# Head sums of k squared as four products of 128 tokens in place of one product of 512 tokens, in a two-layer RWKV-7 and neighbourhood-attention trunk

## Chip, cores and metric

The kernel runs on one core of one Trainium2 chip. The metric is device time in microseconds (us) of one execution; lower is better. The time before is a median of 1630.3 us of three runs (1628.93 to 1637.69).

## What is computed

Two sequences of 512 tokens with 1024 channels (16 heads of 64) go through two layers. Layer 0 is bidirectional RWKV-7 time mixing, layer 1 a gated 2-D neighbourhood attention. The change lies in the first lines of layer 0, where `k` is scaled and divided by its length, head by head:

```python
k = heads(lerp(1) @ w_k).astype(f32)
...
kk = k * k_k.astype(f32).reshape(N_HEADS, HEAD_DIM)
kk = kk / jnp.maximum(jnp.sqrt(jnp.sum(kk * kk, axis=-1, keepdims=True)), 1e-12)
```

So for each of the 16 heads and each of the 512 tokens one sum of 64 squares is needed. The scan that follows uses `-kk` and `kk * a`:

```python
def step(s, inp):
    r_t, w_t, k_t, v_t, a_t, b_t = inp
    sa = jnp.einsum('bhvk,bhk->bhv', s, a_t)
    s = s * w_t[:, :, None, :] + sa[..., None] * b_t[:, :, None, :] + v_t[..., None] * k_t[:, :, None, :]
    return s, jnp.einsum('bhvk,bhk->bhv', s, r_t)
```

## The kernel before, in words

Activations lie with channels on partitions: a tile is 128 channels (two heads) by 512 tokens. A float32 weight product is made of three products of float32r halves, so a *column* (128 output channels) is 8 triples of matmuls, one triple for each 128 input channels. Sequence 0 and 1 are called s = 0 and s = 1, and p = 0..7 counts the columns of a weight.

**The head sums.** `column(s, "k", p, ps)` takes the finished column of `k` from PSUM, copies it and stores it (L717, L718), squares it with the scale `k_k` on ACT (L726), and then lets TensorE (PE) sum the squares over the partitions of each head: one float32 matmul whose weights are the two columns of `ssel` (a one for each partition of head 0, and of head 1), and whose moving operand is the whole square, 128 x 512 (L730). A float32 matmul runs as two passes, so the trace has two records for each. The result, 2 rows by 512 tokens, lies in a PSUM bank of the tag `pm`; ACT copies it out (L733), and the SP queue stores it in the DRAM buffer `ss` of 16 rows (L736). After p = 7 the 16 x 512 sums are loaded as 128 x 64 (L742), ACT takes the root (L744), DVE bounds it and takes the reciprocal (L746, L747), and SP stores it as `rn` (L749). Every `prep` of that sequence then loads rows of `rn` (L955).

There are 8 such sums for s = 0 and 8 for s = 1, in two quite different places:

- **s = 0** lies before the scan. `run` (L1843, L1844) walks through the columns z and k of sequence 0 and lets the `prelude` of sequence 1 step along. There the Tile framework's scheduler sets the order on each engine. Then come the operands for the first columns of r (`shifted`, L1846).
- **s = 1** lies inside `scan_phase`, under a manual schedule for PE, DVE and ACT. There a program of the kernel's own, `weave` (L1703), sets the order at build time. It holds some 15 threads (generators): the recurrence (64 *steps*; each todo n, that is a sequence and four heads, has 8 of them), `preps`, `elimination` and `merges` (they make the inverse matrices of one todo), `finish`, and `flow`. `flow` feeds a long list of weight columns that the scan doesn't depend on at once, to fill PE: `products` (L887 to L889), with their loads, splits and operands, in the groups r, v of s = 0, k of s = 1 (here the head sums), low-rank and z of s = 1, r and v of s = 1, w_o of s = 0, the rest of z, and the first 24 columns of w_in. A triple of L887, L888, L889 is called a filler here; 672 of them are in the scan.

`weave` picks the next instruction by a planner, the class `Clock`: it holds a time for each engine and a cost for each instruction (`matmul` for PE, `scalar` for ACT), and takes the thread of best rank among those that could start now. Where none can start for over 300 ns (`WARM`) and PE was planned busy for under 70% of the last 3.4 us (`cool`), it puts in a *spare* matmul (L1729), whose result nobody reads and which keeps the TensorE clock up. So a change in the cost of one instruction can change the order of all that follows. The recurrence of todo n starts a step with L1277 and then waits, in its first step, until the inverse of todo n is there: that is in steps 9, 17, 25, 33, 41 and 49, and in these waits PE has nothing but fillers, preps and spares.

A group's operands are eight pairs of tiles (`act`, 18 buffers of half a pair each), so the pairs of the next group can only be made as the last column of a group gives its own back. The first column of a group therefore waits on ACT and DVE (L832, L834; in the last group L844 to L872).

Of the kernel before, what the change touches and what calls it, by code (L numbers as in the profile page):

```python
# [13 lines left out]
AF = mybir.ActivationFunctionType  # L14
# [5 lines left out]
P = 128  # L20
T = 512
# [21 lines left out]
CC = {}  # L43
# [7 lines left out]
class Clock:  # L51
# [41 lines left out]
    def room(self, key, bufs):  # L93
        s = self.slots.get(key, ())
        return 0.0 if len(s) < bufs else min(self.left(n) for n in s)
# [88 lines left out]
    def matmul(self, i, ins, n, t):  # L184
        f32, tr = ins[0].dtype == F32, bool(i.is_transpose)
        ts, tp = tuple(i.tile_size), tuple(i.tile_position)
        if not f32:
            c = 0.4375 * n + 3
        elif tr:
            c = 0.84 * n + 2  # L190
        elif ts == (128, 128):
            c = max(1.73 * n + 1, 100.0)
        else:
            c = max(53.0, 0.875 * n + 2)
        if self.mode != ts and self.tiles:
            t = max([t] + [x + 100.0 for x in self.tiles.values()])
            self.tiles = {}
        full = ts == (128, 128)
        if full and not tr and self.mode not in (None, ts):
            c += 104.0  # L200
        elif not full and self.mode == (128, 128):
            t += 48.0
        self.mode = ts
        for (r, q), x in self.tiles.items():
            if r == tp[0] or q != tp[1]:
                t = max(t, x)
        self.tiles[tp] = t + c
        self.t["P"] = t + (13.0 if f32 and not tr else 6.5)
        return t, t + c + self.LAT["P"]
# [44 lines left out]
class Trunk:  # L254
# [111 lines left out]
    def consts(self):  # L366
        nc, cp = self.nc, self.cp
        self.cc = cp.tile([P, NCC], F32, tag="cc", name="cc")
        nc.sync.dma_start(self.cc, self.a["const"])
        c = lambda n, w: self.cc[:, CC[n]:CC[n] + w]  # L370
        self.ident, self.bones, self.ssel = c("ident", 128), c("bones", 128), c("ssel", 2)
        if self.SUMS:
            self.bones = cp.tile([P, 128], F32R, tag="sel", name="sel")
            nc.scalar.copy(self.bones, c("bones", 128))
        self.mstrict, self.mr = c("mstrict", 64), (c("mr", 64), self.cc[:, CC["mr"] + 64:CC["mr"] + 128])
        self.scan = (c("scan", T), self.cc[:, CC["scan"] + 1:CC["scan"] + 1 + T])
        w = c("win", 64)
        self.lower = bass.AP(tensor=w.tensor, offset=w.offset + 31, ap=[list(w.ap[0]), [-1, 32], [1, 32]])
        self.ones = cp.tile([P, P], F32, tag="ones", name="ones")
        nc.vector.memset(self.ones, 1.0)  # L380
        self.one = self.ones[:, 0:1]
        self.dv = dv = cp.tile([P, 136], F32, tag="dv", name="dv")
        v = lambda n, w, o=0: self.cv[:, CV[n] + o:CV[n] + o + w]
        ts = nc.vector.tensor_scalar
        ts(dv[:, 0:16], v("w0", 16), 0.5, None, op0=ALU.mult)
        ts(dv[:, 16:32], v("a0", 16), -0.5, None, op0=ALU.mult)
        ts(dv[:, 32:40], v("ka", 8), -0.5, None, op0=ALU.mult)
        ts(dv[:, 40:48], v("ka", 8), -0.5, 1.0, op0=ALU.mult, op1=ALU.add)
        ts(dv[:, 48:56], v("bin", 8), 0.125, None, op0=ALU.mult)
        ts(dv[:, 56:64], v("bin", 8, 24), 0.5, None, op0=ALU.mult)  # L390
        ts(dv[:, 64:72], v("bin", 8, 16), 0.5, None, op0=ALU.mult)
        ts(dv[:, 72:80], v("lnw", 8), 0.5, None, op0=ALU.mult)
        ts(dv[:, 80:88], v("lnb", 8), 0.5, None, op0=ALU.mult)
        ts(dv[:, 88:112], v("mu", 24), 0.5, None, op0=ALU.mult)
        ts(dv[:, 112:136], v("mu", 24), -1.0, 1.0, op0=ALU.mult, op1=ALU.add)
# [296 lines left out]
    def column(self, s, kind, p, ps):  # L692

        nc, sp = self.nc, self.sp
        vt, act = nc.vector, nc.scalar
        first = lambda e: (e, None, lambda c, n=ps.tensor.name: c.at([n]))
        keep, whole = self.clock.keep, ps.tensor.name
        if kind == "z":

            o, th = self.tmp(), self.tmp()  # L700
            if s == 0:
                yield first("D")
                vt.tensor_tensor(o, ps, self.rstd0, op=ALU.mult)
                ps = o
            yield "A" if s == 0 else first("A")
            keep.add(whole)
            act.activation(th, ps, AF.Tanh, scale=0.5)
            yield "D"
            keep.discard(whole)
            vt.scalar_tensor_tensor(o, th, 1.0, ps, op0=ALU.add, op1=ALU.mult)  # L710
            self.save("z", s, p, o)
            return
        yield "A", None, lambda c: max(c.at([ps.tensor.name]), min(c.room(("tmp", id(self.main)), self.NTMP), 1e10))
        o = self.tmp()
        if kind == "k":
            keep.add(whole)
        act.copy(o, ps)  # L717
        self.save(kind, s, p, o)  # L718
        if kind == "r":
            self.made.add((kind, s, p))  # L720
            return
        if kind == "k":
            yield "A"
            keep.discard(whole)
            sq = self.tmp()
            act.activation(sq, ps, AF.Square, scale=self.vec("kk", p))  # L726
            free, room = self.bank()
            yield "P", free, lambda c: max(room(c), c.at([sq.tensor.name]))
            ss = self.p("pm", (2, T))
            nc.tensor.matmul(ss, self.ssel, sq, start=True, stop=True)  # L730
            yield "A"
            row = self.tmp((2, T))
            act.copy(row, ss)  # L733
            if p == 0:
                sp["ss", s] = self.dram(f"ss{s}", (16, T))
            self.load(sp["ss", s][2 * p:2 * p + 2], row)  # L736
            self.made.add((kind, s, p))
            if p == NP - 1:
                yield "S", None, lambda c: c.at([sp["ss", s].tensor.name])

                rn = self.tmp((P, 64))
                self.load(rn, sp["ss", s].rearrange("a (b c) -> (a b) c", b=8))  # L742
                yield "A"
                act.activation(rn, rn, AF.Sqrt)  # L744
                yield "D"
                vt.tensor_scalar(rn, rn, 1e-12, 2.0 ** 0.5, op0=ALU.max, op1=ALU.mult)  # L746
                vt.reciprocal(rn, rn)  # L747
                sp["rn", s, 0] = self.dram(f"rn{s}", (16, T))
                self.load(sp["rn", s, 0].rearrange("a (b c) -> (a b) c", b=8), rn)  # L749
                self.made.add(("rn", s))  # L750
            return

        if p == 0:

            sp["vt", s] = self.dram(f"vt{s}", (4, 2, NCH // 2, 2, L, 2, 2, HD))
        yield "A"
        back = self.tmp()
        act.copy(back, o[:, ::-1])
        for d in range(2):
            free, room = self.bank()  # L760
            yield "P", free, lambda c: max(room(c), c.at([back.tensor.name]))
            vp = self.p("pm")
            for m in range(4):
                nc.tensor.transpose(vp[:, m * P:(m + 1) * P], (back if d else o)[:, m * P:(m + 1) * P], self.ident)
            yield "A", None, lambda c: max(c.at([vp.tensor.name]), c.room(("vs", id(self.main)), self.NVS))
            vs = self.t("vs", (P, 4, P), self.NVS)
            act.copy(vs, vp.rearrange("p (m c) -> p m c", m=4))
            for j in range(2):
                self.store("vt").dma_start(
                    sp["vt", s][p // 2, j, :, :, :, d, p % 2].rearrange("m h t c -> t (m h) c"),  # L770
                    vs[64 * j:64 * j + 64].rearrange("t m (h c) -> t (m h) c", h=2))
        self.made.add((kind, s, p))
# [1249 lines left out]
```

## Time and profile before

| | |
|---|---|
| median of 3 runs | 1630.3 us |
| profiled execution, device time | 1627.3 us |
| its span, first to last instruction | 1625.5 us |
| granted TensorE clock, mean | 0.981 of full |
| PE busy, 18748 matmul records | 1533.3 us, 94% of the span |
| DVE busy | 1218.4 us, 75% |
| ACT busy | 983.7 us, 61% |
| data moved | 340.46 MB, mean 209 GB/s |
| L1729 spares | 124 records, 62 matmuls |

All times in the text on the profile are of this one execution. A row of a timeline reads: start in us, us from the first start to the last end, engine, line, operation, output <- inputs, tile size (rows*columns of the array), shape, count, and in brackets the idle time before it and who ended it. A row of a table by stretches gives for each engine the busy time and (x) the records, then the granted TensorE clock, the share of the DMA engines and GB/s.

### The profile page before, as it was taken

To read this page: it belongs to the slowest core of one execution; us is meant where nothing else is said; L and a number is where in the kernel's file an instruction comes from. 1 tells how busy PE (TensorE), PEld (TensorE's weight loads), DVE (VectorE), ACT (ScalarE), POOL (GpSimd) and SP (SyncE) were. 2 spreads that over 40 slices of the span, in tenths; PEclk is the share of its full clock that TensorE was granted. 3 is DMA by queue.
4 is the path that set the end of the run, shared out by engine and by line. 5 is a ranking of instruction groups with operands and counts; after the bars stand their busy time and mean duration, and the time that the engine had idled before them with its cause. 6 is when DMAs were issued, how large, how long until landed. Compare 5 with 4: busy or idle time off the path is not lost.

```text
span 1625.5 us, 46341 instructions
## 1 busy us (share of the span) xinstructions
PE 1533.3 (94%) x18748; PEld 1178.7 (73%) x18748; DVE 1218.4 (75%) x2714; ACT 983.7 (61%) x1949; POOL 179.2 (11%) x336
## 2 busy tenths in 40 slices
PE   7989999899989998988999999999999999999998
PEld 6866776666667676766677777777777788777776
DVE  8986587689778787876899998656676575754664
ACT  6567565757648456675666655544667665555562
POOL 0001124201011012231000011000000002100000
PEclk9989999999899999999999999999999999999999
DMA  6447687867576777677776775567664256645553
GB/s 242 158 169 260 212 279 237 270 195 245 167 251 227 239 248 218 224 242 242 247 262 212 233 262 180 160 191 245 196 226 155 93 162 223 224 165 185 163 162 104
DMA packets 182006, 340.46 MB, mean 209 GB/s; under 512 B 25344, under 2 KB 58240, under 8 KB 181792
## 3 DMA queue, kind: packets, MB, share of 16 engines
q1 hardware_dynamic: 158144, 256.75, 49.5%
q0 software_dynamic: 23648, 80.76, 13.9%
q8 instruction: 147, 2.41, 0.6%
q14 instruction: 67, 0.55, 0.1%
HBM read 230.33 MB, written 107.09 MB: 208 GB/s over the span
## 4 chain that ended last, share of the span: by engine, by line
PE 70%; DVE 11%; DMA 7%; issue 5%; ACT 5%; SPq 1%; DVEq 0%; POOL 0%; ACTq 0%; POOLq 0%
PE pm L887 8%; PE pg L454 7%; PE pg L455 6%; PE pg L456 6%; PE pm L888 6%; PE pm L889 6%; PE pf L1199 3%; DMA dab<-ab 2%; PE sc L1537 2%; PE po L1570 2%; PE us L1318 2%; PE pt L1555 2%; PE zy L1271 2%; PE us L1298 2%; DVE ab L1021 1%
## 5 line engine op out<-in xcount | busy, mean ns | idle before, releaser
L887 PE MATMUL pm<-act,whi 128*128 128x512 f32 x672 | 294.6, 438 | 2.7 <-ACT act L832 1.0
L888 PE MATMUL pm<-act,whi 128*128 128x512 f32 x672 | 268.0, 399 | 7.7 <-DVE act L834 6.8
L889 PE MATMUL pm<-act,wlo 128*128 128x512 f32 x672 | 267.3, 398 | 6.6 <-DVE wlo L808 6.6
L887 PEld LDWEIGHTS pm<-act,whi 128*128 128x128 f32 x672 | 127.7, 190 | 45.3 <-issue 12.2
L454 PE MATMUL pg<-act,whi 128*128 128x512 f32 x384 | 160.3, 418 | 0.0
L889 PEld LDWEIGHTS pm<-act,wlo 128*128 128x128 f32 x672 | 128.1, 191 | 37.2 <-DVE wlo L808 8.5
L888 PEld LDWEIGHTS pm<-act,whi 128*128 128x128 f32 x672 | 128.4, 191 | 33.9 <-DVE act L834 11.8
L455 PE MATMUL pg<-act,whi 128*128 128x512 f32 x384 | 152.8, 398 | 0.0
L456 PE MATMUL pg<-act,wlo 128*128 128x512 f32 x384 | 152.3, 397 | 0.0
L404 DVE TENSOR_TENSOR wlo<-raw,whi 128x512 fp32r<-128x512 f32 x148 | 101.6, 689 | 56.1 <-ACT whi L403 55.7
L403 ACT CAST whi<-raw 128x512 fp32r<-128x512 f32 x148 | 91.7, 619 | 83.0 <-PE pg L455 64.9
L808 DVE TENSOR_TENSOR wlo<-raw,whi 128x512 fp32r<-128x512 f32 x168 | 114.6, 684 | 29.1 <-ACT whi L806 29.1
L806 ACT CAST whi<-raw 128x512 fp32r<-128x512 f32 x168 | 103.8, 621 | 45.7 <-PE pm L888 39.5
L456 PEld LDWEIGHTS pg<-act,wlo 128*128 128x128 f32 x384 | 72.2, 188 | 14.9 <-issue 0.3
L454 PEld LDWEIGHTS pg<-act,whi 128*128 128x128 f32 x384 | 72.3, 188 | 14.4 <-issue 3.3
L1098 DVE TENSOR_TENSOR N<-etmp,N 128x30 f32<-128x30 f32 (+14 forms) x240 | 78.9, 329 | 4.6
L455 PEld LDWEIGHTS pg<-act,whi 128*128 128x128 f32 x384 | 72.5, 189 | 13.5 <-issue 2.8
L1096 DVE TENSOR_TENSOR etmp<-N 128x30 f32<-128x30 f32 (+14 forms) x240 | 78.8, 328 | 4.6
L1199 PE MATMUL pf<-cab 64*64 64x128 f32 (+1 forms) x2048 | 68.5, 268 | 6.3 <-issue 5.9
L1551 ACT ACTIVATE sb<-sb,mx 128x256 f32<-128x256 f32 x128 | 64.5, 506 | 11.4 <-DVE mx L1550 10.4
L1548 DVE CUSTOM_DVE_ANT_0 sb<-sc,bias 128x256 f32<-128x256 f32 x128 | 50.1, 420 | 24.3 <-PE pt L1555 13.3
L1310 ACT COPY X<-us 64x256 f32<-64x256 f32 x128 | 47.1, 368 | 33.5 <-PE zy L1177 31.7
(391 smaller groups left out, 3531.3 us busy)
## 6 DMA issues: line engine op xcount, KB each, us to landing
dab<-ab POOLq DMA_DIRECT2D x32, 1024.0 KB, 7.4
cab<-dab SPq DMA_DIRECT2D x64, 512.0 KB
raw<-in_w_in_dram SPq DMA_DIRECT2D x128, 256.0 KB
bias<-in_rpb_dram SPq DMA_DIRECT2D x32, 384.0 KB
raw<-in_w_z_dram SPq DMA_DIRECT2D x32, 256.0 KB
raw<-in_w_k_dram SPq DMA_DIRECT2D x32, 256.0 KB
raw<-in_w_r_dram SPq DMA_DIRECT2D x32, 256.0 KB
k<-dk SPq DMA_DIRECT2D x32, 256.0 KB
```

Of the source, the lines that this page charges most:

```text
L403: self.nc.scalar.copy(hi, src)
L404: (eng or self.nc.vector).tensor_tensor(lo, src, hi.bitcast(F32), op=ALU.subtract)
L454: nc.tensor.matmul(ps, hi, x[k][0], start=(k == 0), stop=False)
L455: nc.tensor.matmul(ps, hi, x[k][1], start=False, stop=False)
L456: self.mm = nc.tensor.matmul(ps, lo, x[k][0], start=False, stop=(k == KT - 1))
L806: nc.scalar.copy(hi, raw[h])
L808: nc.vector.tensor_tensor(lo, raw.pop(h), hi.bitcast(F32), op=ALU.subtract)
L887: nc.tensor.matmul(ps, hi[:, at], xh, start=(k == 0), stop=False)
L888: nc.tensor.matmul(ps, hi[:, at], xl, start=False, stop=False)
L889: nc.tensor.matmul(ps, lo[:, at], xh, start=False, stop=(k == KT - 1))
L1098: vt.tensor_tensor(N[:, q + 1:, :q], tv, N[:, q + 1:, :q], op=ALU.add)
L1199: end = nc.tensor.matmul(st.f[half(a), h, 0, d, g] if st.last else st.f[half(a), h, :, d, g], ab[half(h), d, g, 2 * e[d] + 1 - a], rt if s ...
```

## The change

The weights become 32 columns of the constant `bones` (0.5 where partition and column belong to the same head): columns 48 to 79, 16 of head 0 and 16 of head 1. The square is cut into four pieces of 128 tokens, and each piece gets its own matmul, whose 32 result rows go to PSUM partitions 32j to 32j+31; so four column groups of the array are used in place of one. The PSUM tile and the copy become 128 x 128, SP's store takes every 16th row (8 rows of 128 tokens) and puts them back in token order, and the missing factor 2 goes into the scale of the root. `Clock.matmul` gets a new case, too: a matmul in a 128 x 32 tile is costed like one in a full tile (1.73 ns per token of a row, at least 100), no longer by 0.875 ns per token. The constant `ssel` stays in the table, unused.

```diff
@@ Clock.matmul
-        elif ts == (128, 128):
+        elif ts in ((128, 128), (128, 32)):
             c = max(1.73 * n + 1, 100.0)
         else:
             c = max(53.0, 0.875 * n + 2)
@@ Trunk.consts
-        self.ident, self.bones, self.ssel = c("ident", 128), c("bones", 128), c("ssel", 2)
+        self.ident, self.bones, self.ssel = c("ident", 128), c("bones", 128), self.cc[:, CC["bones"] + 48:CC["bones"] + 80]
@@ Trunk.column
-            ss = self.p("pm", (2, T))
-            nc.tensor.matmul(ss, self.ssel, sq, start=True, stop=True)
+            ss = self.p("pm", (P, P))
+            for j in range(4):
+                nc.tensor.matmul(ss[32 * j:32 * j + 32], self.ssel, sq[:, j * P:(j + 1) * P], start=True, stop=True)
             yield "A"
-            row = self.tmp((2, T))
+            row = self.tmp((P, P))
             act.copy(row, ss)
             if p == 0:
                 sp["ss", s] = self.dram(f"ss{s}", (16, T))
-            self.load(sp["ss", s][2 * p:2 * p + 2], row)
+            self.load(sp["ss", s][2 * p:2 * p + 2].rearrange("a (j t) -> j a t", j=4), row[0:P:16])
@@ after the last p
-                act.activation(rn, rn, AF.Sqrt)
+                act.activation(rn, rn, AF.Sqrt, scale=2.0)
```

The order of instructions shows how the change moves the program. (Lines behind L730 have a number higher by one in the changed kernel: its L888 is L887 of before, its L1730 is L1729.) On PE in the k columns of sequence 0, before:

```order
L456 MATMUL zy_1041<-act_964,wlo_1038 128x512
L730 MATMUL pm_1021<-tmp_1019,cc 2x512
L454 MATMUL zy_1122<-act_915,whi_1114 128x512
L455 MATMUL zy_1122<-act_914,whi_1114 128x512
L456 MATMUL zy_1122<-act_915,wlo_1115 128x512
```

And now:

```order
L456 MATMUL zy_1044<-act_964,wlo_1041 128x512
L731 MATMUL pm_1021<-tmp_1019,cc 32x128 x4
L454 MATMUL zy_1128<-act_915,whi_1120 128x512
L455 MATMUL zy_1128<-act_914,whi_1120 128x512
L456 MATMUL zy_1128<-act_915,wlo_1121 128x512
```

Here nothing moved on PE: four matmuls stand where one stood. In the scan the order differs from the first head sum of s = 1 on. The largest difference stands at the first column of the last group, w_in, that is at the 481st to 488th filler. Before, PE reaches it in steps 44 to 46, with the recurrence between its triples (its last triple, and what follows):

```order
L1199 MATMUL pf_13030<-cab_418_1582 64x2x64 x16
L887 MATMUL pm_12817<-act_13003,whi_12634 128x512
L888 MATMUL pm_12817<-act_13002,whi_12634 128x512
L889 MATMUL pm_12817<-act_13003,wlo_12635 128x512
L1318 MATMUL us_13013<-X_12810,Tm_13008 64x64 x8
L1322 MATMUL zy_12966<-X_12810,R_13005 64x64 x8
```

Now PE reaches it in step 49, while the recurrence waits for the inverse of todo 6, and its last triples stand between spares (L1730) and the products of a prep (L978, L979):

```order
L1730 MATMUL zy_13348<-cc 128x256 x3
L978 MATMUL pm_13441<-h_1419_7116,w2h_13336 128x512
L979 MATMUL pm_13441<-h_1419_7116,w2l_13335 128x512
L1730 MATMUL zy_13348<-cc 128x256
L978 MATMUL pm_13450<-h_1443_7285,w2h_13336 128x512
L979 MATMUL pm_13450<-h_1443_7285,w2l_13335 128x512
L1730 MATMUL zy_13348<-cc 128x256 x9
L888 MATMUL pm_13382<-act_13494,whi_13082 128x512
L889 MATMUL pm_13382<-act_13493,whi_13082 128x512
L890 MATMUL pm_13382<-act_13494,wlo_13083 128x512
L1730 MATMUL zy_13348<-cc 128x256 x5
```

So the boundary between the last two groups moved out of the steps into a wait, and 19 spares were planned there (one more follows behind these rows). In the whole program the spares go from 62 to 87.

## The prediction, made before the changed kernel ran

> **What bounds the kernel now.** I read the page's busy times and its chain first, then the head sums by their lines, then the timeline around them, and last the long waits of the scan by stretches.
>
> ```profile
> PE 1533.3 (94%) x18748; PEld 1178.7 (73%) x18748; DVE 1218.4 (75%) x2714; ACT 983.7 (61%) x1949; POOL 179.2 (11%) x336
> PE 70%; DVE 11%; DMA 7%; issue 5%; ACT 5%; SPq 1%; DVEq 0%; POOL 0%; ACTq 0%; POOLq 0%
> ```
>
> PE is the bound over the whole: busy 94%, and 70% of the chain that ends last. So the time can be written as PE's useful work plus PE's lost time (idle, spares, half clock). The change must be judged by both. The head sums themselves:
>
> ```profile
> L730 PEld LDWEIGHTS pm<-tmp,cc x32: 80/82/84, 103.2 to 407.0; 128*2 128x2 f32 x32
> L730 PE MATMUL pm<-tmp,cc x32: 591/592/1061, 103.2 to 407.4; 128*2 128x512 f32 x32
> L733 ACT COPY tmp<-pm 2x512 f32<-2x512 f32 x16 | 9.2, 573 | 11.5 <-PE pm L730 11.5
> ```
>
> All 32 passes lie between 103 and 408 us. A pass is 592 ns long, but passes overlap, so what one sum takes from PE is read from the starts around it. Four rows of the timeline at the second sum of s = 0:
>
> ```profile
> 107.02 0.39 PE L454 MATMUL zy<-act,whi 128*128 128x512 f32 x1
> 107.25 0.39 PE L455 MATMUL zy<-act,whi 128*128 128x512 f32 x1
> 107.56 1.02 PE L730 MATMUL pm<-tmp,cc 128*2 128x512 f32 x2
> 108.51 0.50 PE L454 MATMUL zy<-act,whi 128*128 128x512 f32 x1
> 108.85 0.40 PE L455 MATMUL zy<-act,whi 128*128 128x512 f32 x1
> ```
>
> Neighbours start every 0.23 us (107.02 to 107.25). From 107.25 to 108.85 are 1.60 us where two such gaps would be 0.46: the sum costs PE 1.14 us. Its two passes start 1.02 - 0.59 = 0.43 apart, so 0.86 is streaming of 2 x 512 tokens, and 0.28 is the way into the small tile and out of it.
>
> **The four products.** Whether they run side by side can be read from other lines of this kernel:
>
> ```profile
> 301.01 1.06 PE L1199 MATMUL pf<-cab 64*64 64x128 f32 x32
> ...
> 1211.47 1.09 PE L1570 MATMUL po<-pts,vtok 128*64 128x128 f32 x16
> 1212.49 1.13 PE L1537 MATMUL sc<-k,q 64*128 64x256 f32 x8
> 1213.56 0.87 PE L1555 MATMUL pt<-cc,sb 128*128 128x128 f32 x6
> ```
>
> The length of one pass of each, from the rows by line:
>
> ```profile
> L1199 PE MATMUL pf<-cab x2048: 218/269/418, 250.5 to 1090.5; 64*64 64x128 f32 x163, 64*64 64x64 f32 x24
> ```
>
> ```profile
> L1570 PEld LDWEIGHTS po<-pts,vtok x512: 132/137/137, 1151.4 to 1585.1; 128*64 128x64 f32 x171
> L1570 PE MATMUL po<-pts,vtok x512: 272/273/324, 1151.4 to 1585.2; 128*64 128x128 f32 x171
> ```
>
> ```profile
> L1555 PE MATMUL pt<-cc,sb x256: 270/272/329, 1142.0 to 1579.1; 128*128 128x128 f32 x128
> ```
>
> L1555 fills the array: 6 passes of 128 tokens, each 0.27 long, start over 0.87 - 0.27 = 0.60, or 0.12 each. L1570 writes two column groups in turn: 16 passes start over 0.82. As 8 pairs that is 0.117 a pair; one after the other it would be 0.05 a pass, which no pass of 128 tokens has here. L1199 uses four tiles, and its 32 passes start over 0.79: eight fours, 0.113 each. So a slot of about 0.115 us takes one pass from each tile. Four column groups are not in the trace, but two and a two-by-two are, and I take two slots: 2 x 0.115 = 0.23, plus 0.28 for in and out, is 0.51 us in place of 1.14. Bounds: in pairs (four slots) 0.74, one after the other (eight) 1.2. So a sum gains 0.63 us, with ends 0.40 and -0.06.
>
> Each pass has a weight load of its own. Sixteen loads of L1570, of 137 ns, would be 2.2 us in a row, and the call took 1.02 (1211.47 to 1212.49); so loads hide behind passes. The Trainium skill, "TensorE: Matmul & The Clock Gate", Part 3, section "The mechanism", says otherwise: a load overlaps a running matmul only where its row group is another one, and four column tiles share their rows. By that rule eight loads of 82 ns would stand between the passes, a sum would cost 0.28 + 0.23 + 0.66 = 1.17, and nothing would be gained; the trace's call of L1570, also in one row group, speaks against it.
>
> **ACT.** The copy goes from 2 x 512 to 128 x 128. The nearest rows:
>
> ```profile
> L1283 ACT COPY Z<-zy 128x256 f32<-128x256 f32 x64 | 23.9, 373 | 38.2 <-PE zy L1277 37.8
> ...
> L1005 ACT COPY wc<-e 128x8 f32<-128x8 f32 x32 | 6.2, 193 | 0.0
> ```
>
> Between 193 ns at 8 elements and 373 at 256, 128 is about 280: 0.29 us less for each of 16. ACT is busy 61%; this counts only where ACT is the next in line (below). The root with a scale costs nothing: it is the same instruction. SP's store has 8 rows of 512 bytes where it had 2 of 2 KB, at most some tenths of a us, on a path only for the last p of each sequence. I put it at nothing.
>
> **s = 0, before the scan.**
>
> ```profile
> 100.00:140.00 40.00, 37.68 (x148) 25.36 (x148) 30.26 (x47) 27.69 (x49) 1.81 (x1) 1.00 0.80 275
> ...
> 147.65 1.87 PE L730 MATMUL pm<-tmp,cc 128*2 128x512 f32 x2 [3.73 <-ACT tmp L726]
> 149.45 4.61 PE L1729 MATMUL zy<-cc 128*128 128x256 f32 x12
> 149.56 0.58 ACT L733 COPY tmp<-pm 2x512 f32<-2x512 f32 x1 [0.32 <-PE pm L730]
> ```
>
> PE is busy 37.68 of 40 us, but the DMA engines are at 0.80, more than in any of the scan's waits below (0.66 to 0.74), so PE's 7 x 0.63 = 4.4 us may be eaten by weights that come late. The last sum ran at half clock after an idle PE: 1.87 us would become about half of that. But behind it PE runs spares until 153.7: it waits for the operands of the first r column, which ACT and DVE make one after the other, not for the sum. There ACT is next in line, and it gains 2 x 0.29. So s = 0 gains between 0.6 us (ACT alone) and 5 us; I take 2.5.
>
> **s = 1, in the scan.** Eight sums at 0.63 are 5.0 us less work for PE. That is all of it that the edit says itself. But the planner puts 87 spares in place of 62, 25 more, and none of these 25 lies ahead of the first sum of s = 1. What a spare stands for is read from the six long waits, from the L1277 of steps 9, 17, 25, 33, 41 and 49 to that of the next step (PE, PEld, DVE, ACT, POOL busy, clock, DMA):
>
> ```profile
> 356.20:433.30 77.10, 71.26 (x802) 49.31 (x806) 65.00 (x126) 48.27 (x86) 9.88 (x17) 0.91 0.67 215
> 487.90:528.10 40.20, 39.68 (x656) 31.59 (x660) 35.65 (x54) 32.68 (x60) 7.26 (x12) 1.00 0.69 226
> 578.50:645.80 67.30, 61.17 (x850) 46.52 (x853) 55.38 (x100) 41.51 (x78) 12.30 (x20) 0.95 0.73 239
> 696.20:741.90 45.70, 39.45 (x597) 30.04 (x599) 34.47 (x57) 32.82 (x59) 14.31 (x22) 0.96 0.66 210
> 799.80:874.70 74.90, 70.27 (x839) 53.78 (x842) 69.81 (x134) 50.48 (x84) 6.98 (x11) 0.98 0.74 247
> 925.80:999.00 73.20, 71.72 (x913) 56.97 (x916) 69.11 (x130) 45.00 (x79) 11.40 (x19) 1.00 0.70 227
> ```
>
> The same six stretches, L1729 alone:
>
> ```profile
> 356.20:433.30 77.10, 4.31 (x16) 2.86 (x16) 0.91 0.67 215
> 487.90:528.10 40.20, 0.00 (x0) 0.00 (x0) 1.00 0.69 226
> 578.50:645.80 67.30, 7.83 (x28) 6.16 (x28) 0.95 0.73 239
> 696.20:741.90 45.70, 2.49 (x10) 1.81 (x10) 0.96 0.66 210
> 799.80:874.70 74.90, 4.55 (x14) 3.13 (x14) 0.98 0.74 247
> 925.80:999.00 73.20, 0.00 (x0) 0.00 (x0) 1.00 0.70 227
> ```
>
> Four waits hold spares: 68 records, 34 spares, 19.2 us. In the same four PE is idle (the stretch less PE's busy time) for 5.8, 6.1, 6.3 and 4.6 us and its clock falls to 0.91 to 0.98. The two waits without spares lose 0.5 and 1.5 us in all, at full clock. So a spare marks a place where PE has nothing to do. The reason shows in the third wait, at a boundary of groups:
>
> ```profile
> 611.56 2.75 PE L1729 MATMUL zy<-cc 128*128 128x256 f32 x12
> ...
> 615.18 0.50 PE L888 MATMUL pm<-act,whi 128*128 128x512 f32 x1 [0.64 <-DVE act L834]
> ...
> 618.94 0.50 PE L888 MATMUL pm<-act,whi 128*128 128x512 f32 x1 [1.08 <-DVE act L834]
> ```
>
> The first column of a group waits for its operands, which ACT and DVE make pair by pair. Between steps the recurrence covers that; in a wait nothing does. In the changed order the boundary of the last group moves out of steps 44 to 46 into the wait of step 49, the one that lost 1.5 us. A filler not done there isn't lost, but is done after the scan, when PE is full: lost PE time counts in full. At 19.2 / 34 = 0.56 us a spare, 25 are 14 us. Bounds: nothing, if the chip's waits are shorter than the planner's, and with the idle of those four waits (19.2 + 22.8) / 34 = 1.24 us, or 31. I take 14, the time of the spares alone, since some idle is there without them.
>
> **The sum.** -2.5 (s = 0) - 5.0 (s = 1) + 14 = +6.5 us. The profiled execution took 1627.3 us, 3.0 below the median of 1630.3; on it the sum gives 1633.8, on the median 1637. A measurement of this kernel can tell about 0.5%, 8 us, from no change, so +6.5 is most likely within it, near its edge.
>
> **The rivals.**
> - *The gain stays, the planned waits don't come.* The planner now costs a sum at four full tiles in turn, above what I expect the chip to need, so PE runs ahead of its plan in s = 1, and fillers that it had planned too late come in time. For it: the edit's gain is certain work, the spares are only planned. Against it: in the waits of before, spares and true idle go together. It gives -5.0 and between -2.5 and -6 (s = 0 with PE and ACT in full): 7.5 to 11 below 1630.3, or 1619 to 1623.
> - *The starved waits cost in full.* One mechanism: the last group's boundary in the wait of step 49. Each spare brings the idle and the half clock of before, 1.24 us: +31 - 7.5, or 1654. It decides from about 0.62 us a spare (15.5 us, which with 7.5 of gain is 8 us slower). For it: 22.8 us of idle in just those waits; against it: waits elsewhere in the new order hold fewer spares.
> - *The change doesn't do what it says.* Loads or column groups run in turn, a sum costs 1.2 us as before, only ACT gains (0.6): 14 - 0.6 = +13, or 1644. Against it speak L1570 and L1199.
>
> **How the numbers follow.** The forecast has 0.44, with a range of its own from +2 to +11 (1632 to 1641); about a third of it is over +8. The first rival has 0.28, half of it beyond -8; the second 0.18, the third 0.08, and 0.02 stays for the rest. Faster by over 0.5%: some 0.18. Within 0.5%: 0.30 of the forecast and 0.11 of the first rival, 0.41. Slower: 0.14 + 0.18 + 0.08 and the rest, 0.41. The range goes from the first rival's 1620 to 1650, which leaves out the upper half of the second rival and a little below.
>
> **What would show it.** Right: eight L730 records a sum, starting in two groups some 0.11 us apart, with 0.5 to 0.6 us lost between neighbours in place of 1.14; a copy of about 0.28 us; some 174 records of L1729, a cluster of them at the first w_in column in the wait of step 49, and PE idle in that wait several us above 1.5. Wrong: records of a sum one behind the other (third rival); waits of steps 17 to 49 that together lose no more than the 44 us (19.2 + 24.8 idle) of before (first rival).

## The result, and the profile after

The changed kernel takes 1658.95 us (median of 4 runs, 1656.88 to 1660.99), beside 1631.54 us for the kernel before (4 runs, 1628.93 to 1637.69): a ratio of 1.015 with a 95% interval of 1.0118 to 1.0183. It is slower, and lies above the predicted range. The profiled execution took 1657.72 us, its span 1655.9 us at a mean clock of 0.974 (before: 1627.3, 1625.5 and 0.981), so the two spans differ by 30.4 us.

The page of the changed kernel, busy times and shares of the chain:

```profile
PE 1543.8 (93%) x18894; PEld 1195.8 (72%) x18894; DVE 1221.3 (74%) x2714; ACT 976.6 (59%) x1949; POOL 178.8 (11%) x336
PE 69%; DVE 9%; DMA 9%; ACT 6%; issue 5%; POOL 0%; SPq 0%; DVEq 0%; ACTq 0%; POOLq 0%
```

PE is still the bound. It is busy 10.5 us longer, though its useful work became less, and it is idle for 112.1 us (1655.9 - 1543.8) where it was idle for 92.2.

**The sums.** First the line of the sums in the changed kernel (duration in ns, shortest, median and longest; first and last start in us), and that of the copy behind them:

```profile
L731 PEld LDWEIGHTS pm<-tmp,cc x128: 105/108/153, 102.7 to 410.9; 128*32 128x32 f32 x128
L731 PE MATMUL pm<-tmp,cc x128: 272/296/422, 102.7 to 411.0; 128*32 128x128 f32 x128
```

```profile
L734 ACT COPY tmp<-pm x16: 243/265/285, 103.2 to 419.2; 128x128 f32<-128x128 f32 x16
```

Then PE's timeline of the changed kernel at the second sum of s = 0, the place that the prediction shows of before:

```profile
106.15 0.39 PE L455 MATMUL zy<-act,whi 128*128 128x512 f32 x1
106.47 0.43 PE L731 MATMUL pm<-tmp,cc 128*32 128x128 f32 x8
106.82 0.50 PE L454 MATMUL zy<-act,whi 128*128 128x512 f32 x1
107.16 0.39 PE L455 MATMUL zy<-act,whi 128*128 128x512 f32 x1
```

From 106.15 to 107.16 are 1.01 us, and less two gaps of 0.23 the sum costs PE 0.55 us, where it cost 1.14. Eight passes of 0.27 to 0.30 us and eight loads of 0.11 fit into 0.35 us (106.47 to 106.82). In the raw records of this sum the eight passes start at 0, 8, 14, 21 and 134, 141, 148, 155 ns: two slots of four. The loads of the second four start at 28 to 48 ns and take 110 ns, while the first passes run (0 to 297 ns): they hide behind passes, and not only behind one another. Sixteen sums so give PE 16 x 0.59 = 9.4 us. The Trainium skill, "TensorE: Matmul & The Clock Gate", Part 3, "The mechanism", lists that a load overlaps a running matmul only in another row group, though the section also names the background weight buffer as a way to load ahead. These four tiles share their rows, and eight loads of 108 ns (0.86 us) went into 0.35 us, so the measurement speaks against that "only" here.

**The six waits.** The same kind of table as in the prediction, for the changed kernel, from the L1278 of steps 9, 17, 25, 33, 41 and 49 to the next step's (PE, PEld, DVE, ACT, POOL busy, clock, DMA share, GB/s):

```profile
358.80:434.90 76.10, 64.60 (x829) 48.10 (x833) 59.20 (x107) 45.96 (x86) 9.77 (x17) 0.91 0.68 210
487.90:548.50 60.60, 56.25 (x717) 42.85 (x720) 57.03 (x108) 37.17 (x67) 8.83 (x15) 0.97 0.69 224
599.70:615.60 15.90, 14.36 (x425) 10.96 (x428) 12.59 (x20) 11.04 (x21) 2.00 (x3) 1.00 0.79 254
692.10:754.50 62.40, 52.68 (x827) 41.34 (x830) 46.74 (x85) 38.36 (x74) 20.22 (x31) 0.92 0.69 223
811.10:871.30 60.20, 52.11 (x698) 40.68 (x701) 50.12 (x89) 41.58 (x70) 4.48 (x7) 0.91 0.74 235
925.10:1009.30 84.20, 76.74 (x806) 60.15 (x810) 80.98 (x159) 48.44 (x83) 8.69 (x14) 0.96 0.55 186
```

And of them the spares alone (L1730; PE and PEld):

```profile
358.80:434.90 76.10, 4.01 (x12) 2.54 (x12) 0.91 0.68 210
487.90:548.50 60.60, 5.70 (x20) 4.30 (x20) 0.97 0.69 224
599.70:615.60 15.90, 0.00 (x0) 0.00 (x0) 1.00 0.79 254
692.10:754.50 62.40, 7.86 (x32) 6.26 (x32) 0.92 0.69 223
811.10:871.30 60.20, 2.92 (x12) 2.27 (x12) 0.91 0.74 235
925.10:1009.30 84.20, 10.58 (x38) 8.04 (x38) 0.96 0.55 186
```

PE is idle in them for 359.4 - 316.7 = 42.7 us (the stretches less their PE column), and 31.1 us go to spares: 73.7 us lost, where it was 44.0. The waits of steps 9, 17, 33, 41 and 49 all lose more than before, only that of step 25 less. Step 49, which had no spare and 1.5 us of idle, has 19 spares and 7.5 us of idle now. What it waits for stands in its timeline:

```profile
932.24 0.50 PE L890 MATMUL pm<-act,wlo 128*128 128x512 f32 x1 [1.93 <-DVE wlo L809]
...
936.43 0.50 PE L979 MATMUL pm<-h,w2l 128*128 128x512 f32 x1 [1.47 <-DVE w2l L967]
...
937.66 4.05 PE L1730 MATMUL zy<-cc 128*128 128x256 f32 x18
943.02 0.51 PE L888 MATMUL pm<-act,whi 128*128 128x512 f32 x1 [1.31 <-ACT act L857]
943.85 0.50 PE L889 MATMUL pm<-act,whi 128*128 128x512 f32 x1 [0.33 <-DVE act L859]
```

After 18 records of spares in 4.05 us (0.45 us a spare) PE still waits 1.31 us for the operands of the last group (L857, then L859).

**The tail.** The fillers that are left when step 64 starts are done at its end. Their first products, L888 after and L887 before, over the stretch from the start of step 64 to the end of the span, the changed kernel first:

```profile
1106.10:1655.90 549.80, 33.02 (x81) 15.22 (x81) 1.00 0.53 176
```

```profile
1094.70:1625.50 530.80, 21.98 (x53) 9.95 (x53) 1.00 0.54 177
```

Step 64 starts 11.4 us later, and 28 more fillers make the stretch behind it 19.0 us longer (0.68 us each): together the 30.4 us. That says where the time shows, not what caused it: at the start of step 49 the two kernels are level (925.1 and 925.8), but 17 fillers have been done less (478 for 495).

As an account of PE: idle +19.9 us; 25 more spares at 0.45 us, +11; the lower clock, 0.026 x 1655.9 less 0.019 x 1625.5, +12; the sums, -9.4. That makes an estimate of +34 for the 30.4 measured. It is a list of where PE's time went, not of prices: one kernel below runs at the same mean clock of 0.974 and is faster than before.

### The profile page after: what moved, and what is told of

Read it like the earlier page. It is cut to its first block, busy times and chain, and to the rows that moved or that the text cites. A ratio compares the mean times of both kernels' runs of the same rounds, so it can differ in the third digit from the quotient of the medians.

```text
span 1655.9 us, 46653 instructions
## 1 busy us (share of the span) xinstructions
PE 1543.8 (93%) x18894; PEld 1195.8 (72%) x18894; DVE 1221.3 (74%) x2714; ACT 976.6 (59%) x1949; POOL 178.8 (11%) x336
## 4 chain that ended last, share of the span: by engine, by line
PE 69%; DVE 9%; DMA 9%; ACT 6%; issue 5%; POOL 0%; SPq 0%; DVEq 0%; ACTq 0%; POOLq 0%
PE pm L888 7%; PE pg L454 6%; PE pg L455 6%; PE pg L456 6%; PE pm L890 6%; PE pm L889 6%; PE pf L1200 3%; DMA dab<-ab 3%; PE sc L1538 2%; PE po L1571 2%; PE us L1319 2%; PE zy L1272 2%; PE us L1299 2%; PE pt L1556 2%; PE zy L1323 2%
## 5 line engine op out<-in xcount | busy, mean ns | idle before, releaser
L888 PE MATMUL pm<-act,whi 128*128 128x512 f32 x672 | 297.2, 442 | 5.7 <-ACT act L857 1.3
L888 PEld LDWEIGHTS pm<-act,whi 128*128 128x128 f32 x672 | 129.1, 192 | 49.5 <-issue 11.9
L890 PEld LDWEIGHTS pm<-act,wlo 128*128 128x128 f32 x672 | 129.2, 192 | 41.2 <-DVE wlo L809 11.9
L1223 DVE TENSOR_TENSOR AK<-zy,cc 128x256 f32<-128x256 f32 x63 | 26.6, 422 | 67.6 <-PE zy L1178 65.3
L1552 ACT ACTIVATE sb<-sb,mx 128x256 f32<-128x256 f32 x128 | 64.2, 503 | 11.9 <-DVE mx L1551 10.9
```

The costliest lines, as they stand in the source:

```text
L888: nc.tensor.matmul(ps, hi[:, at], xh, start=(k == 0), stop=False)
L890: nc.tensor.matmul(ps, lo[:, at], xh, start=False, stop=(k == KT - 1))
```

## The experiments

Two things change at once: the products, and the order that the planner makes of their new costs. The theory after the result: the order costs the time, and the products themselves are a gain. The rival: the products cost something that a count of PE's slots doesn't show. Every ratio below is against the kernel before, with its 95% interval. Every kernel does the reference's work in full; one of them leaves out the spares, and one does the head sums twice.

### New sums in the order of before

Its edit to the changed kernel tells the planner the old costs, so that PE's order in the scan is that of before, row by row, with four products for one:

```diff
+            if e == "P" and tuple(i.tile_size) == (128, 32) and tuple(i.tile_position)[1] < 96:
+                continue
...
+        if ap.tensor.name in self.small:
+            rows, n = (0, 2), 512
...
+        n = 512 if ts == (128, 32) else n
...
-        elif ts in ((128, 128), (128, 32)):
+        elif ts == (128, 128):
```

(`small` holds the names of the copied rows.)

> The four products of the change, with the planner told the costs of the old sum: on PE the order is that of the kernel before, row for row, with 62 spares. If the order of the scan costs the time (theory), the gain of the sums is left: 0.6 us for each of 16 on PE, of which 5 to 8 us count, 1623 to 1628. If the four products themselves hurt (rival: loads, drains, PSUM or the store with 8 rows), the time is near that of the change, 1650 to 1660.

Measured: 1632.74 us (before: 1633.7), 0.9992 (0.9969 to 1.0016). The loss is gone with the order, so the products don't slow the kernel. But the gain that was expected isn't there: 7.5 us would have been 0.9954, outside the interval. The stretch from step 1 to step 10, in which the eight sums of s = 1 lie, before and then in this kernel:

```profile
252.60:433.30 180.70, 166.62 (x2662) 121.33 (x2666) 142.69 (x279) 115.65 (x222) 34.71 (x56) 0.95 0.71 226
```

```profile
256.30:438.50 182.20, 165.23 (x2711) 123.73 (x2714) 141.68 (x278) 113.04 (x222) 34.61 (x56) 0.93 0.71 224
```

PE is busy 1.4 us less, and the stretch is 1.5 us longer, at a lower clock.

### Old sums in the order of the change

The other half, as an edit to the kernel before: one product of 512 tokens, but the planner is told the cost of four of 128.

```diff
+        if ap.tensor.name in self.small:
+            rows, n = (0, 128), 128
...
+        if ts == (128, 32):
+            c = 1.73 * 128 + 1
+            t += 3 * c
```

> The old sum of one product, with the planner told the costs that it has in the change: on PE the order is that of the changed kernel, with 87 spares. Theory (the order costs the time): as slow as the change and 5 to 8 us more for the dear sums, 1662 to 1668. Rival (the products hurt): near before, 1630 to 1635.

Measured: 1674.88 us, 1.0242 (1.0208 to 1.0277). The order alone slows the kernel before by more than the whole change does, and by more than the 1662 to 1668 that was expected. Within this order the new sums are worth 1.0242 / 1.0150, 0.9%.

### The change without its case in the planner

```diff
-        elif ts in ((128, 128), (128, 32)):
+        elif ts == (128, 128):
```

> The change without its line in the planner, so that a product in a 128 x 32 tile is costed at 114 ns each and not at 222. The order is a third one, with 68 spares, and 628 fillers are done when the last step of the scan starts (619 before, 591 in the change). Theory: 6 spares more than before at 1.4 us each (27 us and some 7 us of gain, over 25 spares) less 7 us of gain: about 1632, 1626 to 1638. Rival (products hurt): 1650 to 1660.

Measured: 1649.32 us, 1.0091 (1.006 to 1.0122). This order has 68 spares, six more than before. Spares at any price of the prediction don't explain 15 us: the expectation failed.

### The planner's case alone

The reverse of that line, in the kernel before and nothing else:

> The old sum of one product, with the line in the planner alone, which then costs it at 887 ns and not at 450. A fourth order, with 74 spares and 640 fillers at the start of the last step. By spares at 1.4 us each 12 more than before would be +17 us, 1648; if what counts is how many fillers are left for the end (32, with 53 before and 81 in the change), it would be at or under before, 1615 to 1632. Rival (products hurt): 1631, as before.

Measured: 1663.28 us, 1.0183 (1.0139 to 1.0226), with 74 spares and only 32 fillers left for the tail. Neither spares at 1.4 us each (1648) nor fillers left (1615 to 1632) give this time. One line in the planner's table of costs, with not one instruction of the program's work changed, costs 1.8%.

### The change, with other costs told to the planner

So which number of the order tells its time? The planner's own clock at the last instruction of the scan, which the kernel's build works out (not a time of the chip), was my next candidate; the rivals were the count of spares and that of fillers left. I took three costs of a sum whose orders lie apart by these three measures. For 300 ns, as an edit to the changed kernel:

```diff
+            if e == "P" and tuple(i.tile_size) == (128, 32) and tuple(i.tile_position)[1] < 96:
+                continue
...
-        elif ts in ((128, 128), (128, 32)):
+        elif ts == (128, 128):
...
+        if ts == (128, 32):
+            c = 300.0
```

> The four products, with the planner told 300 ns for a sum in all (the trace shows 0.55 us with the way in and out, of which the planner adds 0.15 by itself) and the true shape of the copy. The order has 55 spares, 49 fillers left behind the start of the last step (before 53, the change 81), and the planner's own clock, which is part of the kernel and no chip time, ends its scan at 973.8 us, with 978.6 before, 991.3 without the planner's line and 1001.9 in the change. Theory A (the order decides, and the planner's own end tells how good it is): 4.8 below before, and a sum that costs no more than planned: 1622 to 1630. Theory B (the order decides, but by chance that the planner doesn't see; before is a lucky one): 1640 to 1660 like the others.

Measured: 1627.25 us (before: 1636.46, 20 runs), 0.9933 (0.991 to 0.9956). This version beats both kernels.

The same with `c = 650.0`:

> The four products, with the planner told 650 ns for a sum and the true shape of the copy. 53 spares, the fewest of all; the planner's own clock ends at 977.4. Theory A (planner's end): about as before, 1628 to 1636. By spares (1.4 us each): 9 fewer, 1615 to 1622. Theory B (chance): 1640 to 1660.

Measured: 1627.96 us, 0.9943 (0.9921 to 0.9964), at a mean clock of 0.974. That is at the lower edge of theory A, but faster than "about as before", and not as fast as spares at 1.4 us would have it.

The first experiment's kernel with `c = 500.0` added, where it had 0.875 x 512 + 2 = 450:

> The four products, with the planner told 500 ns for a sum and the old shape of the copy: 50 ns more than in the run that kept the order of before, nothing else. That already gives another order, with 72 spares; the planner's own clock ends at 986.8, 8.2 above before. Theory A: 1637 to 1645. By spares (10 more at 1.4 us): 1645 to 1650. If orders were alike: 1632.

Measured: 1647.81 us, 1.0075 (1.0047 to 1.0103). The time lies in the range of the spares and above that of theory A; by the ratio it is 12 us above the kernel before, where A had 8.2 in the planner's time and the spares 14. So this run doesn't decide between them. Fifty nanoseconds in the plan of the 8 sums of s = 1 (the planner sees no others) are worth 0.8% of the kernel. The six kernels with new sums, sorted by the planner's own end:

| planner told of a sum | planner's end of the scan, us | ratio to before | spares | fillers left |
|---|---|---|---|---|
| 300 ns | 973.8 | 0.9933 | 55 | 49 |
| 650 ns | 977.4 | 0.9943 | 53 | 53 |
| old costs (450 ns) | 978.6 | 0.9992 | 62 | 53 |
| old costs, 500 ns | 986.8 | 1.0075 | 72 | 49 |
| no case (four of 114 ns) | 991.3 | 1.0091 | 68 | 44 |
| the change (four of 222 ns) | 1001.9 | 1.0150 | 87 | 81 |

(A new build of the changed kernel ends its plan at 999.8; 1001.9 is the figure of the expectation above. The rank is the same.) The planner's end sorts all six medians. By spares two pairs stand the wrong way round, 55 and 53, 68 and 72; but in both pairs the intervals of the ratios overlap, so these six don't tell the planner's end from the count of spares: both rank the orders. Fillers left don't (49 stands at 0.9933 and at 1.0075). The ends differ by 28 and the times by 2.2%, some 35 us, so the planner's end is no forecast of the time.

### The change without its spares

Do the spares hold up useful work that is ready? Here the order is that of the change, but its 87 spares, which nobody reads, are left out; the planner still counts them.

```diff
-                self.nc.tensor.matmul(self.spare, self.ident, self.scan[0][:, 0:256], start=not did["states"], stop=True, skip_group_check=True)
```

> The changed kernel in its own order, with the spare matmuls left out (their result is read by nobody); the planner still counts them. If the spares only fill time in which PE has nothing to do (theory), the time stays near 1659 or rises, as the clock falls more often: 1655 to 1690. If the spares themselves keep real work waiting (rival), 25 of them weigh at least 11 us: 1635 to 1650.

Measured: 1675.82 us, 1.0229 (1.0196 to 1.0261), at a clock of 0.956 (0.974 with them). On balance they hold up no useful work; without them it is 0.8% worse. The waits of steps 33 and 49 in this kernel:

```profile
696.90:759.90 63.00, 48.78 (x795) 37.45 (x798) 46.58 (x85) 38.22 (x74) 20.25 (x31) 0.84 0.67 211
...
932.20:1018.80 86.60, 70.67 (x765) 53.02 (x769) 81.17 (x160) 48.85 (x83) 8.72 (x14) 0.87 0.56 190
```

With spares they took 62.4 and 84.2 us at 0.92 and 0.96; without, 63.0 and 86.6 at 0.84 and 0.87. The time that the spares filled is idle now, and what follows it runs slower. In the timeline of this kernel at step 49 one can see it:

```profile
944.73 0.80 PE L979 MATMUL pm<-h,w2l 128*128 128x512 f32 x1 [2.77 <-DVE w2l L967]
...
951.32 0.79 PE L888 MATMUL pm<-act,whi 128*128 128x512 f32 x1 [4.93 <-ACT act L857]
```

The products take 0.8 us where the same two took 0.5. The Trainium skill, "TensorE: Matmul & The Clock Gate", Part 1, "What's actually happening", has the clock's gate follow how busy PE has lately been; the trace agrees (0.974 and 0.956).

### What the sums are worth in the good order

The kernel before with one product of 512, in the order of the 300 ns kernel:

```diff
+        if ap.tensor.name in self.small:
+            rows, n = (0, 128), 128
...
+        if ts == (128, 32):
+            c = 300.0
```

> The old sum of one product in the order of the run whose planner was told 300 ns (on PE the same order in the scan). It parts that run's gain of 0.7%, 11 us, into order and sums. If the order alone makes it (the sums gave nothing in the order of before: 0.9992): 0.992 to 0.997 of before. If the sums bring their 16 x 0.59 = 9.6 us of PE time here: 0.998 to 1.003. If they bring more than their PE time, as the two runs in the slow order suggest (1.024 against 1.015): over 1.003.

Measured: 1642.24 us (before: 1635.06), 1.0052 (1.0032 to 1.0072). Against 0.9933 the new sums bring 1.2%, some 19 us, twice the 9.4 us of PE time. With old sums this order, better by the planner's end (973.8) and with fewer spares (55), is slower than that of before (978.6 and 62). So neither number ranks orders whatever the sums cost. A likely reason, not tested, is that the planner was told 300 ns for a sum that costs 1.14 us here. From step 9 to step 17, first with the new sums and then with the old ones:

```profile
360.40:484.10 123.70, 115.32 (x2092) 85.92 (x2092) 113.50 (x227) 77.39 (x152) 15.73 (x28) 1.00 0.74 241
```

```profile
360.50:494.50 134.00, 122.22 (x2052) 87.57 (x2052) 114.30 (x227) 79.74 (x152) 15.70 (x28) 0.97 0.69 223
```

The two start level, and 10.3 us of the 13.8 between the profiled spans come from here: PE is busy 6.9 us less, idle 3.4 us less (8.4 for 11.8), and its clock stays at 1.00.

### The old sums twice

To cost sum work by itself in the order of before, each old product is issued twice (the second writes the same result again), and the planner sees one:

```diff
...
-            nc.tensor.matmul(ss, self.ssel, sq, start=True, stop=True)
+            for _ in range(2):
+                nc.tensor.matmul(ss, self.ssel, sq, start=True, stop=True)
```

> The kernel before with every sum computed twice (the second product writes the same result again; the planner sees one): 16 x 0.86 = 13.8 us more work for PE, in the scan the order of before. If PE has slack where the sums stand, as the missing gain of the four products in this order suggests: 0.998 to 1.003 of before. If the time of the sums counts in full: 1.007 to 1.010.

Measured: 1653.22 us, 1.0112 (1.0077 to 1.0146). 16 x 0.86 = 13.8 us more of PE's time cost 18 us (13 to 24 by the interval). Step 1 to step 10:

```profile
257.70:450.50 192.80, 177.27 (x2678) 125.58 (x2682) 143.16 (x279) 115.17 (x222) 34.60 (x56) 0.92 0.66 212
```

It is 12.1 us longer than before for eight products of 0.86 us, 6.9 us, in an execution of 1659.2 us, the slowest of the four. So sum work isn't hidden in this order: more of it costs its full price; whether it costs more than that, the interval doesn't tell. That less of it gave nothing (0.9992) stays without an explanation.

## Why the prediction was wrong, step by step

- **A sum on PE, "0.51 us in place of 1.14": right.** It is 0.55, in two slots of four passes, 0.13 apart, with the loads hidden. L1570 and L1199 were the right rows to read it from, and the rival "the change doesn't do what it says" falls with it.
- **ACT's copy, "about 280": right**, 265 ns. SP's store, put at nothing, takes 0.55 us to issue where it took 0.25 (medians of 16); no run parts its price from the rest.
- **The new order as the cost: right in kind.** Old sums in the new order, 1.0242, and new sums in the old one, 0.9992, show it. The 174 records, the starved boundary in step 49 and the fillers done at full price after the scan came as written, and the waits lose 73.7 us, not 44, which is what was to show the first rival wrong.
- **The order's size, "I take 14, the time of the spares alone": wrong; this step sets the miss.** From 0.9992 to 1.0150 the order costs 26 us with the new sums, 1.04 us for each of the 25 spares, not 0.56; with the old sums (1.0242) it costs 40. What the term left out is the idle around the spares, put at nothing since "some idle is there without them": in the six waits spares take 11.9 us more than before, and PE is idle for 17.8 us more, together 29.7 us for 23 more spares, 1.29 each, close to the upper bound of 1.24. The second rival (1654) was nearest, in price; but its one place isn't enough: by idle and spares together step 49 loses 16.6 us more than before, but steps 9, 17, 33 and 41 also lose 5.4, 9.5, 8.8 and 1.8 more, and step 25 loses 12.4 less. That the order costs the time is shown; how much each of these places costs isn't, as no run moved one of them alone.
- **One price for a spare: wrong.** With new sums six more (no case) cost 16 us, ten more (500 ns) 14 and 25 more (the change) 26, against 0.9992; with old sums 12 more (the planner's case alone) cost 30. That is 1.0 to 2.7 us a spare, where the prediction had 0.56. A spare marks a place where the planner expects nothing to do; it doesn't tell how much time is lost there. The planner's own end ranks the six orders with new sums, and the count of spares does so too but for two pairs within their noise; with old sums both put the 300 ns order ahead of the one before, and it is slower.
- **The gain, "-2.5 (s = 0) - 5.0 (s = 1)": wrong in the order of before, too small in others.** 0.1% there, within its interval nothing; 0.9% in the change's order and 1.2% in the 300 ns order. For s = 0 the gain reaches PE in full as far as the first filler, so late weights don't eat it there. The seventh sum, the eighth in the changed kernel and the first filler, before and after:

```profile
142.90 1.02 PE L730 MATMUL pm<-tmp,cc 128*2 128x512 f32 x2
153.71 0.59 PE L887 MATMUL pm<-act,whi 128*128 128x512 f32 x1
```

```profile
138.87 0.43 PE L731 MATMUL pm<-tmp,cc 128*32 128x128 f32 x8
144.27 0.65 PE L731 MATMUL pm<-tmp,cc 128*32 128x128 f32 x8 [4.98 <-ACT tmp L726]
149.74 0.58 PE L888 MATMUL pm<-act,whi 128*128 128x512 f32 x1
```

  The first sums of the two start at 103.2 and 102.7 us, so 3.5 us are gained over six sums, as 6 x 0.59 would have it, and the first filler still starts 4 us earlier (2.9 on the mean of ten executions, 153.6 with old sums and 150.7 with new). What is left of it when the scan begins can't be told: step 1 starts at 254.2 us on the mean of the profiled executions of before and three others with old sums, and at 253.4 in six with new ones, but single ones of them lie between 250.7 and 256.3. For s = 1 the worth of a sum depends on what the order lets PE do with the time. That the worth shrinks to nothing in the one order that was found for old costs is what the ratios show; why is open.
- **The chances: a slip.** Half of the first rival's 0.28 is 0.14 for each side of -8, not 0.17 and 0.11, as the sums of the chances have it; nothing else hangs on it.

## What to carry to other kernels

Where a program at build time chooses the order, an edit to a cost is an edit to everything behind it: keep the products and the order apart, by telling the planner the old cost, before judging either. Compare the planner's own end and its spares for the two orders before any run: here both ranked the orders of the new sums. But neither gave the time, and both failed for the old sums in the 300 ns order, where the planner was told 300 ns for 1.14 us. And an edit that is a gain in itself may need its order chosen anew: the same products went from 1.0150 to 0.9933 with one number in the planner.

## What was not expected of the hardware

- Four column groups of one row group run together: passes start 7 ns apart, in slots of 133 ns for 128 tokens of float32, and eight loads of 108 ns hide behind them. At half clock, in the last sum of s = 0, the two slots lie 214 ns apart.
- Matmuls that nobody reads are worth having: taking 87 of them out cost 0.8% (1.0150 to 1.0229), with the mean clock down from 0.974 to 0.956.
- Time taken off PE is not worth a fixed price: 9.4 us less brought between nothing and 19 us, depending on the order around it, and 13.8 us more cost 18 (13 to 24).
